# Two-layer decoder trunk: distance tables of the dilated heads loaded one head ahead, latent low parts held behind the first head's scores

## The chip, the cores and the metric

The kernel runs on one core of a Trainium2 chip, in one launch. The metric is the device time of one execution in microseconds, the median of three runs. A profile is one further execution that the hardware profiler recorded; its times are used for the working, the median for the comparison.

## The reference

Two layers, each with a hybrid token mixer, a cross-attention into 256 memory tokens and a squared-ReLU MLP, on 512 tokens of 1024 features in f32. Only the mixer is touched by the change. It projects the normed tokens once and uses the columns for two groups of heads:

```python
z = h @ w_in
c_q, c_kv, k_rope = z[..., :o1], z[..., o1:o2], z[..., o2:o3]    # 384, 256 and 32 columns: "latent"
q_d, k_d, v_d = z[..., o3:o4], z[..., o4:o5], z[..., o5:]        # 512 columns each: "dilated"
q = (rms_norm(c_q, q_norm_g) @ w_uq)                             # 8 latent heads, rope on 32 of 96 columns
kv = (rms_norm(c_kv, kv_norm_g) @ w_ukv)
k_pe = rope(k_rope, positions)                                   # shared by the 8 latent heads
o_mla = causal_block_attention(q, k, v_mla)
for window, dil in ((128, 1), (512, 4), (2048, 16)):             # 8 dilated heads
    s = q_d . k_d * scale + rel_bias[t5_bucket(distance)]        # only the keys of that window and dilation
    o_p, lse_p = softmax(s) @ v_d, logsumexp(s)
o_dil = sum_p softmax_p(lse_p) * o_p
return concat([o_mla, o_dil]) @ w_out
```

## The kernel before

**Numbers.** Every f32 matmul is three fp32r passes: the high part of one operand times the low part of the other, low times high, high times high (L239, L240 and L241). A weight tile `raw`, which SP loads from memory (L157), is therefore split before use: ACT writes the high part `whi` (L192) and VectorE the low part `wlo` as raw minus high (L197). The pools hold 8 raw tiles and 5 each of whi and wlo, so ACT's next `whi` waits until TensorE has done the matmuls of the fifth tile before it.

**The dilated heads.** For a pair of query and key the three dilations together depend on the distance alone, so one table of 128 x 512 per head, `tb`, holds the bias and the count of dilations. The tables are built once, written to memory (`tabw`), and each head loads its own (`dil_table`, L691, 256 KB). `scores` (L460) takes a head in four steps of 128 queries and 128, 256, 384 and 512 keys: TensorE writes `sp` (L467, two passes: keys' high part `kh` and low part `kl`, against a query tile `qs` that holds both parts), VectorE adds the table and takes the row maximum (`P` and `nm`, L471), ACT takes the exponential (L473), VectorE the reciprocal `rs` (L474), POOL scales (L475). There are two PSUM buffers for `sp`, so the third step's matmul waits until VectorE has done the first step. `transposed_scores` transposes P on TensorE (`ptp`, L224), ACT and VectorE copy it out (`PT`, L494 and L492), and `weighted_values` multiplies a pair of heads by the values (`op`, L230).

**The order.** In each layer the q and k columns of the dilated heads are projected feature by feature (`feat_major`, tiles `pfm`; four 128-feature tiles of k, 8 x 3 matmuls each). Each k tile is evacuated for two heads: `kh` on ACT (L637), `kl` on VectorE (L641), and POOL copies both into the other 64 rows (L643). Then `attention()` runs the heads, and `weave` lets the generators `latent()` and `memory()` put their work between its steps, by a ratio of TensorE time: the projection of c_kv and k_rope (`ptm` of 288 columns), of c_q (`ptm` of 384 columns), then the transposes `ctp` and the latent heads' own projections. There are four PSUM buffers for `pfm` and `ptm` together. Within an engine the instructions stand in an order that the scheduler of the compiler's tile framework sets from the program's order and its estimates; `tc.issue_after(x)` makes it put instructions behind x there. All loads stand in one queue of SP, and a load that waits for a free `raw` tile holds those behind it.

Of the kernel before, what the change touches and what calls it, by code (L numbers as in the profile page):

```python
# [11 lines left out]
F32 = mybir.dt.float32  # L12
# [8 lines left out]
S = 512  # L21
# [24 lines left out]
def block_kernel(ctx: ExitStack, tc, x, mem, positions, rel_bias, w_in, q_norm_g, w_uq, kv_norm_g,  # L46
# [11 lines left out]
    sm = ctx.enter_context(tc.tile_pool(name="sm", bufs=40))  # L58
# [109 lines left out]
    def load_w(src, r0, kts, c0, width, gcol=None, heads=0):  # L168
# [18 lines left out]
        for k in range(kts):  # L187
            g = 1.0 if gcol is None else gT[:, gcol + k:gcol + k + 1]
            loads[0] += 1

            with tc.issue_after(token_parts[0]) if 3 <= loads[0] <= 8 else nullcontext():
                weight_parts[:] = [nc.scalar.activation(cols(hi, k, False), cols(raw, k, True), AF.Copy, scale=g).ins]  # L192
            if not SPLIT:
                continue
            lv, rv, hv = cols(lo, k, False), cols(raw, k, True), cols(hi, k, False).bitcast(F32)
            for lv, rv, hv in [(lv[:, e], rv[:, e], hv[:, e]) for e in range(2)] if heads else [(lv, rv, hv)]:
                nc.vector.scalar_tensor_tensor(lv, rv, g, hv, op0=OP.mult, op1=OP.subtract)  # L197
# [256 lines left out]
    OFFS = [0, 128, 384, 768]  # L454

# [3 lines left out]
    def scores(P, parts, tb, scale):  # L459
# [3 lines left out]
        for i in range(NT):  # L463
            L = 128 * (i + 1)
            sp = pss.tile([128, 512], F32, tag="s", name="sp")
            for n, (q, k) in enumerate(parts):
# [4 lines left out]
            nc.vector.tensor_tensor_reduce(out=Pi, in0=sp[:, :L], in1=tb[:, 512 - L:512], scale=-scale,  # L471
                                           scalar=3e38, op0=OP.add, op1=OP.min, accum_out=nm[:, i:i + 1])
# [37 lines left out]
    cs = const.tile([128, NT, 2, ROPE], F32, name="cs")  # L510
    tabd = dr.tile([HEADS, 640], F32, name="tabd")
# [50 lines left out]
    for l in range(DEPTH):  # L562
# [29 lines left out]
        def rope(dst, src, t, n):  # L592

            cosb = cs[:, t, 0:1, :].to_broadcast([128, n, ROPE])
            a = unit("ra")[:, :n * ROPE].rearrange("p (h r) -> p h r", r=ROPE)
            b = unit("rb")[:, :n * ROPE].rearrange("p (h r) -> p h r", r=ROPE)
# [89 lines left out]
        feat_major(wl, o3 + 512, 4, NK, gm, xh_f, xl_f, S, ev_kd, whole=1)  # L686

        def dil_table(h):
            tb = unit("tb")
            src = tabw[h]  # L690
            nc.sync.dma_start(tb, bass.AP(tensor=src.tensor, offset=src.offset + 127, ap=[[639, 128], [1, 512]]))  # L691
            return tb

# [5 lines left out]
        def latent():  # L699
# [3 lines left out]
            yield from tok_major_steps(wl, 0, QL, NK, gm, xh_t, xl_t, NT, ev_cq, whole=True)  # L703
            rq = rstd_from(ssq, QL, "rq")
# [138 lines left out]
        def attention():  # L843

            P, PTs = [None] * 16, [None] * 16
            for i in range(17):
                if i < 8:
                    P[i] = new_scores()
                    yield from scores(P[i], dilated_parts(i), dil_table(i), 1.0)
# [321 lines left out]
```

## Time and profile before

| | |
|---|---|
| median of three runs | 1549.14 us (1545.85 to 1550.41) |
| the profiled execution, its own time | 1551.81 us |
| its span in the trace | 1550.0 us |
| mean granted TensorE clock | 0.989 |
| TensorE, VectorE, ACT, POOL busy | 97%, 64%, 53%, 15% of the span |
| median time of a table from issue to landing | 5.0 us, 16 tables |

Layer 0's dilated heads stand between about 83 and 160 us of the span, layer 1's between about 850 and 925 us. A row of the timeline view gives the start, the duration, the engine, the line and the tile (what is written, `<-`, what is read), and in brackets the idle time of the engine before it with the instruction that ended it. The clock column of a stretch is the share of full speed that the throttle granted TensorE: 1.00 is 2.4 GHz and 0.50 is 1.2 GHz.

### The profile page before, as it was taken

The numbers are of one execution on the slowest core, as the hardware profiler recorded it, in microseconds if no ns is written. First come the engines' busy times: TensorE is split into PE (matmuls) and PEld (weight loads), VectorE is DVE, ScalarE is ACT, GpSimd is POOL, SyncE is SP. The second block draws the span as 40 slices with busy tenths as digits, with TensorE's granted clock in tenths as the row PEclk, the third lists the DMA queues.
The fourth block names the chain that finished last, engine by engine and source line by source line (L and its number), as shares of the span: only waits on it lengthen the run. The fifth ranks groups of instructions, "written<-read, shape, count | busy, mean of one in ns | idle before, by whom it ended". The sixth has DMA issues, their size and how long they took to land.

```text
span 1550.0 us, 21290 instructions
## 1 busy us (share of the span) xinstructions
PE 1509.1 (97%) x7861; PEld 1265.6 (82%) x7861; DVE 995.9 (64%) x1780; ACT 820.0 (53%) x1578; POOL 239.0 (15%) x429
## 2 busy tenths in 40 slices
PE   8999999999999999999989999999999999999996
PEld 7777788898898888888868877978988988888885
DVE  5555775456458668585974667664654594958678
ACT  5355666346346464545554566653553654646363
POOL 2133631021020000000011355201111100000000
PEclk9989999999999999999999999999999999999999
DMA  6432223613131505151541322244322324060612
GB/s 235 143 116 69 79 65 109 204 55 119 53 114 50 181 28 177 41 166 59 179 131 51 122 81 91 69 140 145 109 82 68 115 71 155 17 195 20 190 55 82
DMA packets 87404, 164.09 MB, mean 106 GB/s; under 512 B 6230, under 2 KB 12036, under 8 KB 87300
## 3 DMA queue, kind: packets, MB, share of 16 engines
q1 hardware_dynamic: 86724, 161.68, 32.4%
q8 instruction: 62, 1.02, 0.3%
q10 hardware_dynamic: 576, 1.05, 0.2%
q14 instruction: 42, 0.34, 0.1%
HBM read 154.29 MB, written 11.03 MB: 107 GB/s over the span
## 4 chain that ended last, share of the span: by engine, by line
PE 84%; DVE 7%; issue 3%; ACT 2%; DMA 2%; POOL 1%; SPq 0%; DVEq 0%; POOLq 0%; ACTq 0%
PE pfm L240 12%; PE pfm L239 12%; PE pfm L241 12%; PE ptm L239 6%; PE ptm L240 6%; PE ptm L241 6%; PE wa L239 3%; PE wa L240 3%; PE wa L241 3%; PE sp L467 3%; PE op L230 3%; DVE wlo L197 2%; PE ptp L224 2%; PE wc L240 2%; PE wc L239 2%
## 5 line engine op out<-in xcount | busy, mean ns | idle before, releaser
L240 PE MATMUL pfm<-xth,wlo 128*128 128x512 f32 (+1 forms) x896 | 322.4, 360 | 0.6
L239 PE MATMUL pfm<-xtl,whi 128*128 128x512 f32 (+1 forms) x896 | 322.2, 360 | 0.0
L241 PE MATMUL pfm<-xth,whi 128*128 128x512 f32 (+1 forms) x896 | 321.6, 359 | 0.0
L197 DVE SCALAR_TENSOR_TENSOR wlo<-raw,gT,whi 128x512 fp32r<-128x512 f32 (+3 forms) x332 | 229.1, 729 | 131.6 <-ACT whi L192 129.9
L192 ACT ACTIVATE whi<-raw,gT 128x512 fp32r<-128x512 f32 (+2 forms) x324 | 209.2, 697 | 180.3 <-PE pfm L241 87.3
L164 ACT ACTIVATE whi<-raw 128x1024 fp32r<-128x1024 f32 x112 | 118.1, 1060 | 142.9 <-PE pfm L241 52.8
L240 PEld LDWEIGHTS pfm<-xth,wlo 128*128 128x128 f32 x896 | 169.2, 189 | 26.8 <-DVE wlo L197 1.4
L241 PEld LDWEIGHTS pfm<-xth,whi 128*128 128x128 f32 x896 | 169.2, 189 | 25.6 <-issue 0.5
L239 PEld LDWEIGHTS pfm<-xtl,whi 128*128 128x128 f32 x896 | 169.2, 189 | 24.8
L165 DVE TENSOR_TENSOR wlo<-raw,whi 128x1024 fp32r<-128x1024 f32 x112 | 134.8, 1217 | 34.3 <-ACT whi L164 34.3
L139 POOL TENSOR_TENSOR pnr<-pnm,mhalf 128x1 f32<-128x1 f32 x24 | 18.0, 750 | 828.8 <-DVE pnm L420 828.8
L475 POOL TENSOR_SCALAR P<-P,rs 128x128 f32<-128x128 f32 (+3 forms) x128 | 71.5, 563 | 151.6 <-DVE rs L474 81.2
L239 PE MATMUL wa<-wlo,fh 128*128 128x512 f32 x240 | 93.6, 390 | 0.5 <-DVE acc L1105 0.5
L241 PE MATMUL wa<-whi,fh 128*128 128x512 f32 x240 | 93.4, 389 | 0.0
L240 PE MATMUL wa<-whi,fl 128*128 128x512 f32 x240 | 93.4, 389 | 0.0
L473 ACT ACTIVATE P<-P,nm 128x128 f32<-128x128 f32 (+3 forms) x128 | 71.2, 557 | 34.1 <-DVE nm L471 33.4
L185 DVE TENSOR_TENSOR wlo<-raw,whi 128x1024 fp32r<-128x1024 f32 x32 | 39.1, 1222 | 59.3 <-ACT whi L184 58.6
L239 PE MATMUL ptm<-wlo,xth 128*128 128x512 f32 (+2 forms) x192 | 68.6, 359 | 3.4 <-DVE wlo L197 2.5
L184 ACT ACTIVATE whi<-raw 128x1024 fp32r<-128x1024 f32 x32 | 33.9, 1061 | 67.3 <-PE ptm L241 60.2
L240 PE MATMUL ptm<-whi,xtl 128*128 128x512 f32 (+2 forms) x192 | 67.1, 349 | 0.6 <-DVE xtl L203 0.6
L241 PE MATMUL ptm<-whi,xth 128*128 128x512 f32 (+2 forms) x192 | 66.3, 346 | 0.0
L224 PE MATMUL ptp<-ident,P 128*128 128x128 f32 x320 | 50.5, 282 | 3.9 <-ACT PT L494 2.3
(249 smaller groups left out, 3280.4 us busy)
## 6 DMA issues: line engine op xcount, KB each, us to landing
raw<-in_w_up SPq DMA_DIRECT2D x64, 512.0 KB, 4.6
raw<-in_w_down SPq DMA_DIRECT2D x64, 512.0 KB, 4.3
raw<-in_w_in SPq DMA_DIRECT2D x24, 512.0 KB, 5.5
raw<-in_w_xk SPq DMA_DIRECT2D x16, 512.0 KB, 5.4
raw<-in_w_xv SPq DMA_DIRECT2D x16, 512.0 KB, 3.6
raw<-in_w_mix_out SPq DMA_DIRECT2D x16, 512.0 KB, 4.7
raw<-in_w_xq SPq DMA_DIRECT2D x16, 512.0 KB, 6.4
raw<-in_w_xo SPq DMA_DIRECT2D x16, 512.0 KB, 4.1
```

What stands on the lines that cost most here:

```text
L164: nc.scalar.activation(hi, raw, AF.Copy)
L165: nc.vector.tensor_sub(lo, raw, hi.bitcast(F32))
L192: weight_parts[:] = [nc.scalar.activation(cols(hi, k, False), cols(raw, k, True), AF.Copy, scale=g).ins]
L197: nc.vector.scalar_tensor_tensor(lv, rv, g, hv, op0=OP.mult, op1=OP.subtract)
L224: ins = nc.tensor.transpose(out_, in_, ident_)
L230: nc.tensor.matmul(ps, lhsT=lhsT, rhs=rhs, start=start, stop=stop)
L239: nc.tensor.matmul(ps, lhsT=lh, rhs=rl, start=first, stop=False, skip_group_check=more)
L240: nc.tensor.matmul(ps, lhsT=ll, rhs=rh, start=False, stop=False, skip_group_check=more)
L241: nc.tensor.matmul(ps, lhsT=lh, rhs=rh, start=False, stop=last, skip_group_check=more)
L467: nc.tensor.matmul(sp[:, :L], lhsT=q[:, i * 128:(i + 1) * 128], rhs=k[:, :L], start=n == 0, stop=n == len(parts) - 1)
L473: nc.scalar.activation(Pi, Pi, AF.Exp, bias=nm[:, i:i + 1], scale=-1.0, accum_out=rs[:, i:i + 1])
L475: nc.gpsimd.tensor_scalar(Pi, Pi, rs[:, i:i + 1], 1.0, op0=OP.mult, op1=OP.mult)
```

## The change

Four things, all in the mixer. First, the tables of heads 0 and 1 are loaded ahead of the k projection, and head i (1 to 6) loads the table of head i+1 before its own scores; before, each head loaded its own table ahead of its own scores. Second, from the end of head 0's score steps until the loads of c_q's weights have been put into the program, `behind[0]` holds the last score instruction of head 0, and every `wlo` of a gained weight that is written in that time is put behind it. Third, the rope of the shared key uses a constant tile `rot` instead of two tiles of the pool `un`. Fourth, the pool of small tiles has 34 buffers instead of 40.

```diff
--- before.py
+++ after.py
@@ -55,7 +55,7 @@
     wp = ctx.enter_context(tc.tile_pool(name="wp", bufs=5))
     un = ctx.enter_context(tc.tile_pool(name="un", bufs=39))
     pp = ctx.enter_context(tc.tile_pool(name="pp", bufs=2))
-    sm = ctx.enter_context(tc.tile_pool(name="sm", bufs=40))
+    sm = ctx.enter_context(tc.tile_pool(name="sm", bufs=34))
     psm = ctx.enter_context(tc.tile_pool(name="psm", bufs=4, space=bass.MemoryType.PSUM))
     pss = ctx.enter_context(tc.tile_pool(name="pss", bufs=2, space=bass.MemoryType.PSUM))
     pst = ctx.enter_context(tc.tile_pool(name="pst", bufs=2, space=bass.MemoryType.PSUM))
@@ -194,7 +194,8 @@
                 continue
             lv, rv, hv = cols(lo, k, False), cols(raw, k, True), cols(hi, k, False).bitcast(F32)
             for lv, rv, hv in [(lv[:, e], rv[:, e], hv[:, e]) for e in range(2)] if heads else [(lv, rv, hv)]:
-                nc.vector.scalar_tensor_tensor(lv, rv, g, hv, op0=OP.mult, op1=OP.subtract)
+                with nullcontext() if behind[0] is None else tc.issue_after(behind[0]):
+                    nc.vector.scalar_tensor_tensor(lv, rv, g, hv, op0=OP.mult, op1=OP.subtract)
         return hi, lo
 
     def split_from(hi, lo, src):
@@ -452,6 +453,8 @@
         run(out_proj_steps(*a, **k))
 
     OFFS = [0, 128, 384, 768]
+    score_op = [None]
+    behind = [None]
 
     def new_scores():
         return pp.tile([128, 1280], F32, tag="P", name="P", bufs=2)
@@ -468,8 +471,9 @@
                                  start=n == 0, stop=n == len(parts) - 1)
                 clk[0] += L * (0.00042 if SPLIT else 0.00167)
             Pi = P[:, OFFS[i]:OFFS[i] + L]
-            nc.vector.tensor_tensor_reduce(out=Pi, in0=sp[:, :L], in1=tb[:, 512 - L:512], scale=-scale,
-                                           scalar=3e38, op0=OP.add, op1=OP.min, accum_out=nm[:, i:i + 1])
+            score_op[0] = nc.vector.tensor_tensor_reduce(
+                out=Pi, in0=sp[:, :L], in1=tb[:, 512 - L:512], scale=-scale, scalar=3e38, op0=OP.add,
+                op1=OP.min, accum_out=nm[:, i:i + 1]).ins
             nc.scalar.activation(Pi, Pi, AF.Exp, bias=nm[:, i:i + 1], scale=-1.0, accum_out=rs[:, i:i + 1])
             nc.vector.reciprocal(rs[:, i:i + 1], rs[:, i:i + 1])
             nc.gpsimd.tensor_scalar(Pi, Pi, rs[:, i:i + 1], 1.0, op0=OP.mult, op1=OP.mult)
@@ -508,6 +512,7 @@
         return oh_, ol_
 
     cs = const.tile([128, NT, 2, ROPE], F32, name="cs")
+    rot = const.tile([128, 2, ROPE], F32, name="rot")
     tabd = dr.tile([HEADS, 640], F32, name="tabd")
     tabw = dr.tile([HEADS, 128, 640], F32, name="tabw")
 
@@ -592,8 +597,8 @@
         def rope(dst, src, t, n):
 
             cosb = cs[:, t, 0:1, :].to_broadcast([128, n, ROPE])
-            a = unit("ra")[:, :n * ROPE].rearrange("p (h r) -> p h r", r=ROPE)
-            b = unit("rb")[:, :n * ROPE].rearrange("p (h r) -> p h r", r=ROPE)
+            a, b = (rot[:, 0:1], rot[:, 1:2]) if n == 1 else [
+                unit(name)[:, :n * ROPE].rearrange("p (h r) -> p h r", r=ROPE) for name in ("ra", "rb")]
             nc.gpsimd.tensor_tensor(a, src, cosb, op=OP.mult)
             for e in range(2):
                 nc.gpsimd.tensor_tensor(b[:, :, e * 16:(e + 1) * 16], src[:, :, (1 - e) * 16:(2 - e) * 16],
@@ -683,7 +688,6 @@
             distance_tables()
             rotary_tables()
         feat_major(wl, o3, 4, NK, gm, xh_f, xl_f, S, ev_qd)
-        feat_major(wl, o3 + 512, 4, NK, gm, xh_f, xl_f, S, ev_kd, whole=1)
 
         def dil_table(h):
             tb = unit("tb")
@@ -691,6 +695,10 @@
             nc.sync.dma_start(tb, bass.AP(tensor=src.tensor, offset=src.offset + 127, ap=[[639, 128], [1, 512]]))
             return tb
 
+
+        tables = [dil_table(0), dil_table(1)]
+        feat_major(wl, o3 + 512, 4, NK, gm, xh_f, xl_f, S, ev_kd, whole=1)
+
         ring = [None, None]
         scored = [0]
         keyed, queried = [0], [0]
@@ -701,6 +709,7 @@
             yield from tok_major_steps(wl, QL, KVL + ROPE, NK, gm, xh_t, xl_t, NT, ev_ckv, whole=True)
             rkv = rstd_from(sskv, KVL, "rkv")
             yield from tok_major_steps(wl, 0, QL, NK, gm, xh_t, xl_t, NT, ev_cq, whole=True)
+            behind[0] = None
             rq = rstd_from(ssq, QL, "rq")
             for t in range(NT):
                 nc.vector.tensor_scalar(ckv[t][:, :KVL], ckv[t][:, :KVL], rkv[:, t:t + 1], None, op0=OP.mult)
@@ -846,7 +855,11 @@
             for i in range(17):
                 if i < 8:
                     P[i] = new_scores()
-                    yield from scores(P[i], dilated_parts(i), dil_table(i), 1.0)
+                    if 1 <= i < 7:
+                        tables.append(dil_table(i + 1))
+                    yield from scores(P[i], dilated_parts(i), tables[i], 1.0)
+                    if i == 0:
+                        behind[0] = score_op[0]
                     yield
                 elif i < 16:
                     while min(keyed[0], queried[0]) <= i - 8:
```

What this makes of the order is seen best in three places. The first is ACT in layer 0, from the end of the q projection to the first exponentials of head 0 (`qs` and `kh` are evacuations of the q and k projections, `whi` the high parts of the weights of c_kv, 288 wide, and c_q, 384 wide). Before:

```order
L626 ACTIVATE qs<-pfm 64x512 x3
L637 ACTIVATE kh<-pfm 64x512 x6
L192 ACTIVATE whi<-raw,gT 128x288 x6
L637 ACTIVATE kh<-pfm 64x512
L192 ACTIVATE whi<-raw,gT 128x384 x2
L637 ACTIVATE kh<-pfm 64x512
L192 ACTIVATE whi<-raw,gT 128x384 x6
L473 ACT_TABLE_LOAD
L473 ACTIVATE P,rs<-P,nm 128x128
L473 ACTIVATE P,rs<-P,nm 128x256
```

The same engine at the same place now:

```order
L631 ACTIVATE qs<-pfm 64x512 x3
L192 ACTIVATE whi<-raw,gT 128x288 x6
L192 ACTIVATE whi<-raw,gT 128x384 x2
L642 ACTIVATE kh<-pfm 64x512 x4
L477 ACT_TABLE_LOAD
L477 ACTIVATE P,rs<-P,nm 128x128
L642 ACTIVATE kh<-pfm 64x512
L477 ACTIVATE P,rs<-P,nm 128x256
L477 ACTIVATE P,rs<-P,nm 128x384
L477 ACTIVATE P,rs<-P,nm 128x512
```

The eight `whi` of 288 and 384 columns that stood behind and between the keys' evacuations now stand ahead of all eight `kh`, three of which come after head 0's exponentials; six `whi` of 384 columns, which stood ahead of head 0's exponentials, come later.

VectorE beside it, where `kl` is the keys' low part and `P,nm` the score instruction of head 0. Before:

```order
L628 SCALAR_TENSOR_TENSOR qs<-pfm,qs 64x512 x3
L641 TENSOR_TENSOR kl<-pfm,kh 64x512 x6
L197 SCALAR_TENSOR_TENSOR wlo<-raw,gT,whi 128x288 x6
L641 TENSOR_TENSOR kl<-pfm,kh 64x512
L197 SCALAR_TENSOR_TENSOR wlo<-raw,gT,whi 128x384 x2
L641 TENSOR_TENSOR kl<-pfm,kh 64x512
L197 SCALAR_TENSOR_TENSOR wlo<-raw,gT,whi 128x384 x2
L615 COPY ckv<-ptm 128x288
L197 SCALAR_TENSOR_TENSOR wlo<-raw,gT,whi 128x384 x3
L471 ISA P,nm<-sp,tb 128x128
L471 ISA nm 128x1
L471 ISA P,nm<-sp,tb 128x256
```

And now:

```order
L633 SCALAR_TENSOR_TENSOR qs<-pfm,qs 64x512 x3
L198 SCALAR_TENSOR_TENSOR wlo<-raw,gT,whi 128x288 x6
L646 TENSOR_TENSOR kl<-pfm,kh 64x512 x3
L474 ISA P,nm<-sp,tb 128x128
L474 ISA nm 128x1
L474 ISA P,nm<-sp,tb 128x256
L474 ISA nm 128x1
L646 TENSOR_TENSOR kl<-pfm,kh 64x512
L474 ISA P,nm<-sp,tb 128x384
L474 ISA nm 128x1
L478 RECIPROCAL rs<-rs 128x1
L474 ISA P,nm<-sp,tb 128x512
```

Five low parts of 384 columns stood right ahead of head 0's first score instruction, and two more ahead of those; now the first of them comes behind head 0's last. Three `kl` stand ahead of the first score instruction where all eight stood.

The second place is SP, where `tb` is a table. In layer 0, from the latent heads' up-projection weights (`uq`, `ukv`) to the memory keys' weights (`xk`), before:

```order
L691 DMA tb<-tabw 128x512
L157 DMA raw<-in_w_xk 128x2x512
L691 DMA tb<-tabw 128x512
L157 DMA raw<-in_w_xk 128x2x512 x2
L691 DMA tb<-tabw 128x512 x2
L157 DMA raw<-in_w_xk 128x2x512 x2
L691 DMA tb<-tabw 128x512
L157 DMA raw<-in_w_xk 128x2x512 x2
L691 DMA tb<-tabw 128x512 x2
```

The first `tb` here is head 1's; head 0's stands further ahead. And now, where the first two are those of heads 2 and 3, with heads 0 and 1 further ahead:

```order
L695 DMA tb<-tabw 128x512 x2
L157 DMA raw<-in_w_ukv 128x2x512
L157 DMA raw<-in_w_xk 128x2x512 x3
L695 DMA tb<-tabw 128x512 x2
L157 DMA raw<-in_w_xk 128x2x512 x2
L695 DMA tb<-tabw 128x512
L157 DMA raw<-in_w_xk 128x2x512 x2
L695 DMA tb<-tabw 128x512
L157 DMA raw<-in_w_xk 128x2x512
```

The tables of heads 4 and 5 come behind three loads of `xk`, where head 5's came behind five; those of heads 2 and 3 come ahead of the last `ukv`.

In layer 1 the same stretch, before:

```order
L157 DMA raw<-in_w_uq 128x2x384
L691 DMA tb<-tabw 128x512
L157 DMA raw<-in_w_uq 128x384
L691 DMA tb<-tabw 128x512 x2
L157 DMA raw<-in_w_ukv 128x2x512
L157 DMA raw<-in_w_xk 128x2x512 x3
L691 DMA tb<-tabw 128x512 x2
L157 DMA raw<-in_w_xk 128x2x512 x2
L691 DMA tb<-tabw 128x512
L157 DMA raw<-in_w_xk 128x2x512 x2
```

And now:

```order
L695 DMA tb<-tabw 128x512 x2
L157 DMA raw<-in_w_uq 128x384
L157 DMA raw<-in_w_ukv 128x2x512
L157 DMA raw<-in_w_uq 128x2x384
L695 DMA tb<-tabw 128x512
L157 DMA raw<-in_w_uq 128x384
L695 DMA tb<-tabw 128x512
L157 DMA raw<-in_w_ukv 128x2x512
L157 DMA raw<-in_w_xk 128x2x512 x3
L695 DMA tb<-tabw 128x512 x2
L157 DMA raw<-in_w_xk 128x2x512 x2
```

Head 3's table stood behind `ukv` and three `xk`, and now stands ahead of them (the fourth `tb` of the second piece); head 4's is still behind them.

The third place is TensorE at head 5 of layer 0: `sp` of 384 and 512 keys is the second half of a head's scores, `ctp` the transposes of the latent rows, `ptp` those of P. Before:

```order
L467 MATMUL sp<-kh,qs 128x256
L467 MATMUL sp<-kl,qs 128x256
L224 MATMUL ctp<-ident,ckv 128x128 x4
L224 MATMUL ptp<-ident,P 128x128 x7
L224 MATMUL ctp<-ident,ckv 128x128 x4
L224 MATMUL ctp<-ident,cq 128x128 x4
L467 MATMUL sp<-kh,qs 128x384
L467 MATMUL sp<-kl,qs 128x384
L467 MATMUL sp<-kh,qs 128x512
L467 MATMUL sp<-kl,qs 128x512
L239 MATMUL ptm<-wlo,ch 128x384
L224 MATMUL ctp<-ident,cq 128x128 x4
```

And now:

```order
L470 MATMUL sp<-kh,qs 128x256
L470 MATMUL sp<-kl,qs 128x256
L225 MATMUL ctp<-ident,ckv 128x128 x4
L225 MATMUL ptp<-ident,P 128x128
L470 MATMUL sp<-kh,qs 128x384
L470 MATMUL sp<-kl,qs 128x384
L470 MATMUL sp<-kh,qs 128x512
L470 MATMUL sp<-kl,qs 128x512
L225 MATMUL ptp<-ident,P 128x128 x3
L470 MATMUL sp<-kh,qs 128x128
L470 MATMUL sp<-kl,qs 128x128
L470 MATMUL sp<-kh,qs 128x256
```

The second half of head 5's scores stood behind seven transposes of P and eight of the latent rows, and now stands behind four and one.

## Rows read from the trace of the kernel before

**Rows 1.** Profile page, busy time of each engine, share of the span, instructions
```profile
PE 1509.1 (97%) x7861; PEld 1265.6 (82%) x7861; DVE 995.9 (64%) x1780; ACT 820.0 (53%) x1578; POOL 239.0 (15%) x429
```

**Rows 2.** What PE waited for over the span: total us, times, longest us
```profile
PE sp L467 <- DVE nm L471: 11.4, 11, 1.9
```

**Rows 3.** What VectorE waited for, 85 to 260 us (layer 0), same columns
```profile
DVE P L471 <- DMA tb<-tabw: 2.2, 1, 2.2
```

**Rows 4.** The same for 835 to 935 us (layer 1)
```profile
DVE P L471 <- DMA tb<-tabw: 7.8, 3, 4.1
```

**Rows 5.** Stretches: length, PE, PEld, DVE, ACT, POOL busy, PE clock, DMA share, GB/s
```profile
96.50:98.40 1.90, 0.05 (x2) 0.01 (x1) 1.90 (x7) 1.88 (x3) 0.00 (x0) 1.00 0.57 172
...
99.40:109.60 10.20, 9.20 (x27) 5.91 (x27) 4.50 (x18) 6.04 (x20) 2.09 (x4) 0.50 0.68 214
...
140.00:143.70 3.70, 1.84 (x12) 1.15 (x11) 2.30 (x5) 1.82 (x5) 0.00 (x0) 1.00 0.87 234
143.70:150.60 6.90, 5.52 (x15) 3.71 (x15) 4.20 (x16) 3.47 (x10) 3.12 (x5) 0.51 0.46 179
```

**Rows 6.** ACT in order: start us, us, line, operation, [idle before, releaser]
```profile
67.22 0.59 ACT L637 ACTIVATE kh<-pfm 64x512 fp32r<-64x512 f32 x1 [0.75 <-PE pfm L241]
...
83.48 0.59 ACT L637 ACTIVATE kh<-pfm 64x512 fp32r<-64x512 f32 x1 [0.35 <-PE pfm L241]
83.98 1.11 ACT L192 ACTIVATE whi<-raw,gT 128x384 fp32r<-128x384 f32 x2
...
94.26 3.15 ACT L192 ACTIVATE whi<-raw,gT 128x384 fp32r<-128x384 f32 x6 [8.55 <-issue]
97.42 1.28 ACT L473 ACT_TABLE_LOAD   x1
```

**Rows 7.** VectorE in order, around head 0's first score, same columns
```profile
84.11 0.68 DVE L641 TENSOR_TENSOR kl<-pfm,kh 64x512 fp32r<-64x512 f32 x1 [0.21 <-ACT kh L637]
...
98.05 0.28 DVE L471 CUSTOM_DVE_ANT_0 P<-sp,tb 128x128 f32<-128x128 f32 x1
```

**Rows 8.** POOL in order, 64 to 105 us, same columns
```profile
67.98 0.61 POOL L643 TENSOR_SCALAR kh<-kh 64x512 fp32r<-64x512 f32 x1 [44.10 <-ACT kh L637]
```

**Rows 9.** TensorE in order, third score step of head 0, same columns
```profile
98.39 0.44 PE L467 MATMUL sp<-kh,qs 128*128 128x384 f32 x1 [1.85 <-DVE nm L471]
```

**Rows 10.** TensorE in order, 139 to 152 us, around head 5 of layer 0
```profile
140.79 0.55 PE L224 MATMUL ptp<-ident,P 128*128 128x128 f32 x3 [0.75 <-ACT PT L494]
141.99 0.65 PE L224 MATMUL ctp<-ident,ckv 128*128 128x128 f32 x4 [0.65 <-DVE PT L492]
...
145.08 0.69 PE L467 MATMUL sp<-kh,qs 128*128 128x384 f32 x1 [1.84 <-DVE nm L471]
```

**Rows 11.** DMA issues of SP, 130 to 150 us: start, us, line, tile
```profile
139.63 0.42 SPq L691 DMA_DIRECT2D tb<-tabw  x1
```

**Rows 12.** DMA issues of SP, 872 to 905 us, layer 1
```profile
874.82 4.29 SPq L157 DMA_DIRECT2D raw<-in_w_xk  x3
879.16 0.93 SPq L691 DMA_DIRECT2D tb<-tabw  x2
```

**Rows 13.** VectorE in order, 876:900 us, heads 3, 4, layer 1
```profile
885.29 0.29 DVE L471 CUSTOM_DVE_ANT_0 P<-sp,tb 128x128 f32<-128x128 f32 x1 [4.09 <-DMA tb<-tabw]
...
889.48 0.28 DVE L471 CUSTOM_DVE_ANT_0 P<-sp,tb 128x128 f32<-128x128 f32 x1
```

**Rows 14.** Stretches of layer 1, columns as in Rows 5
```profile
857.00:859.00 2.00, 0.86 (x7) 0.63 (x6) 0.43 (x3) 0.09 (x1) 0.00 (x0) 1.00 1.03 379
...
883.00:886.00 3.00, 1.11 (x9) 0.80 (x8) 0.71 (x5) 0.91 (x3) 0.00 (x0) 1.00 0.44 171
886.00:890.00 4.00, 4.00 (x27) 3.86 (x26) 2.85 (x13) 2.86 (x10) 2.15 (x4) 1.00 0.00 0
902.00:908.30 6.30, 3.33 (x25) 2.43 (x23) 4.16 (x11) 3.24 (x8) 0.00 (x0) 1.00 0.85 282
908.30:911.80 3.50, 3.47 (x13) 3.20 (x13) 3.08 (x12) 2.52 (x8) 1.95 (x4) 0.51 0.57 219
```

## The prediction

> **What bounds the kernel.** I read the profile's page first: TensorE is busy for 97% of the span and VectorE for 64% [rows 1]. So only two things can be won: stretches in which TensorE stands idle, and stretches in which it works at the lower granted clock. The list of waits comes next. TensorE's largest single wait is that of a score matmul for VectorE's `nm`, 11.4 us in 11 waits [rows 2]: with two PSUM buffers for `sp`, the third step of a head starts when VectorE has scored the first. VectorE itself waited for a table once in layer 0, for 2.2 us [rows 3], and three times in layer 1, for 7.8 us [rows 4]. Last I read the timelines around these waits and cut the stretches there, for busy time and clock. The change touches five places.
>
> *Layer 0, head 0.* No table is late here. VectorE has five low parts of c_q's weights ahead of the first score. The last ones need high parts that ACT began at 94.26 after 8.55 us of waiting [rows 6], which is the wait for a free `whi` buffer (the word "issue" names no releaser). So the first score starts at 98.05 [rows 7], and TensorE's third step at 98.39 [rows 9]. In 96.5 to 98.4 TensorE worked 0.05 of 1.90 us, so 1.85 are lost; then for 10.20 us the clock is 0.50, with 9.20 busy [rows 5]. That is 1.00 idle, and 9.20 x 0.50 = 4.60 lost to the clock. Sum 7.45 us.
>
> *Layer 0, head 5.* The table is issued at 139.63 [rows 11] behind five loads of `xk`, VectorE waits 2.2 [rows 3], TensorE 1.84 after it [rows 10]. The stretches 140 to 143.7 and 143.7 to 150.6 lose 1.86 and 1.38 idle, and 5.52 x 0.49 = 2.70 by the clock of 0.51 [rows 5]. Sum 5.94.
>
> *Layer 1.* In the stretch of head 0's wait TensorE stood for 2.00 - 0.86 = 1.14, in that of head 3's for 3.00 - 1.11 = 1.89, both at clock 1.00, and at 1.00 in the 4 us behind head 3's [rows 14]. Around head 5 the loss is 6.30 - 3.33 = 2.97 idle and 3.47 x 0.49 = 1.70 by the clock of 0.51 [rows 14], 4.67 in all.
>
> **The change, part by part.** All terms are microseconds won, against the profiled execution (1551.81, span 1550.0).
>
> *The hold, layer 0, head 0.* The low parts of c_q no longer stand ahead of head 0's score, so the wait of 1.85 and what the clock did behind it go: 7.45 won. But the new order puts eight `whi` ahead of all `kh`. Before, the first `kh` ran at 67.22, while TensorE was still in the k projection [rows 6]. Now the last two `whi` of 384 columns wait for a buffer that the last k matmul sets free; its end is about 83.45, by the `kh` of 83.48 that it released [rows 6]. ACT then needs 1.11 for the two [rows 6], so `kh` starts at about 84.6 and the next one 0.50 later (83.48 to 83.98 [rows 6]). POOL's copy starts 0.76 behind `kh` (67.22 to 67.98) and takes 0.61 [rows 6, 8], so it is done at 86.0; `kl` starts 0.63 behind `kh` (83.48 to 84.11) and takes 0.68 [rows 6, 7], and POOL's copy of it is done at about 86.6. Head 0's first scores need both. What stood behind them on TensorE, the c_kv projection, needs a PSUM buffer that head 1's `kl` sets free, at 86.6 as well. So TensorE, which had no gap here, now stands for 86.6 - 83.45 = 3.1. I bound it by 2.5 (only the first pass waits) and 4.0 (one more evacuation of 0.68 and its neighbour in the way). Behind this gap the clock may fall. The nearest rows are at one end the 4.60 of the old gap, at the other 0, which is what layer 1's head 3 showed behind 1.89 idle [rows 14]. I take 1.70, that of layer 1's head 5, where dense work followed as it does here. Short waits in the new softmax of head 0: the old stretch had 1.00, bounds 0 and 1.00, I take 0.6. Won: 7.45 - (3.1 + 1.7 + 0.6) = 2.0, with ends 7.45 - 2.5 = 5.0 and 7.45 - 9.6 = -2.2.
>
> ACT's table load of 1.28 [rows 6] moves ahead, between the keys' evacuations and the first score's arrival; it costs nothing as long as `kl` and the scores take longer than it. If that cover goes, it is part of the 0.6.
>
> *Tables early, layer 0, head 5.* Its table now stands behind three `xk` loads, where head 4's stood, and VectorE's single wait for a table [rows 3] was not for head 4's. So the 1.84 goes. The waits of 0.75 and 0.65 for copies of P's transposes [rows 10] do not depend on a table and stay, and the scores of heads 5 and 6 now stand closer together, behind the same copies: I charge one more wait of 0.75. Of the clock's 2.70 I count half, since idle time remains just ahead. Won: 1.84 - 0.75 + 1.35 = 2.4; ends 1.84 - 1.40 = 0.4 and 1.84 + 2.70 = 4.5.
>
> *Layer 1.* Head 0: the table is there, but its scores now come ahead of low parts that `ptm` needs next; I take 0, between -1.1 and 1.1. Head 3: its table stood behind three `xk` loads that SP issued at 874.82, and went out at 879.16 [rows 12]; VectorE waited 4.09 for it [rows 13]. Now it goes out ahead of them, so all of TensorE's 1.89 is won; ends 0 and 1.9. Head 5: by the same share as in layer 0 (2.4 of 5.94), 4.67 x 0.41 = 1.9; ends 0 and 4.67 - 1.40 = 3.3.
>
> *The rest.* `rot` changes only where POOL's scratch lies; the POOL instructions are as many, and POOL is busy for 15% [rows 1]. Without that cover it would be one POOL instruction of some 0.6 ahead of `ctp`. The smaller pool of small tiles holds fewer of them alive; I see no instruction that it makes wait. Both 0.
>
> *Sum:* 2.0 + 2.4 + 0 + 1.9 + 1.9 = 8.2. The profiled execution would be 1551.81 - 8.2 = 1543.6. It was 2.67 above the median of the runs, 1549.14, so the forecast is **1540.9 us**. With all upper ends (5.0 + 4.5 + 1.1 + 1.9 + 3.3 = 15.8) it is 1533.3, with all lower ends (-2.9) 1552.0. The forecast's own range is 1537 to 1544.5.
>
> **A rule on the queue.** Head 4's table in layer 1 is still issued behind the three `xk` loads. The row shows the issue at 879.16, and the table of the same issue pair landed at 885.29, 6.1 us later [rows 12, 13]. Head 4's first score started at 889.48 [rows 13], that is 4.2 later. The Trainium skill (page "DMA: Bandwidth & Descriptors", section "Two DMAs through the same engine are not ordered") says that within one queue of one DMA engine the descriptors start in order, so a transfer can't begin ahead of those issued before it. The trace agrees with that by those 6.1 us against the page's median of 5.0; by this rule the time would be that of rival 4 if head 4's scores came over 4.2 earlier, and the forecast if not.
>
> **The rivals.**
> 1. *Nothing takes the place of what goes.* The new gap is at its short end and the clock holds everywhere. For it: layer 1's head 3 kept clock 1.00 behind 1.89 idle [rows 14]. Against it: 3.1 is longer than any gap listed for a score [rows 2]. All upper ends: 1549.14 - 15.8 = 1533.3.
> 2. *The clock makes the new gap as dear as the old one.* For it: 1.85 idle were followed by 10.20 us at 0.50 [rows 5]. Against it: there the work behind was a broken chain of scores, here it is a dense projection. Head 0 becomes 7.45 - (3.1 + 4.6 + 1.0) = -1.25, the rest stays 6.2: 4.95 won, 1544.2.
> 3. *The tables were hidden anyway at head 5.* The copies of P and of the latent rows bind there, and head 5 gives 0.4 in layer 0 and nothing in layer 1, while head 0 gives nothing because its gap eats it: 0.4 + 1.9 = 2.3, so 1546.8. For it: the waits of 0.75 and 0.65 [rows 10]. Against it: a clock of 0.51 behind these gaps [rows 5, 14].
> 4. *The wait moves from head 3 to head 4 in layer 1.* Table 4 lands no earlier; 1.9 less is won: 1542.8. Against it: the 4.2 us of room.
> 5. *Slower: late evacuations hold PSUM.* Five of the keys' evacuations now stand among or behind head 0's exponentials on ACT, and each projection of c_kv's rows needs one of four PSUM buffers that they set free. If the scheduler's estimates are off, TensorE waits there again, for the second and third rows, each time as long as the first (3.1), with the clock at 0.50 in between: 3 x 3.1 + 4.6 + 1.0 = 14.9 against 7.45, and of the rest only 0.4 + 1.9 stays. That is 5.2 lost, 1554.3. It decides once the loss at head 0 passes 7.45 + 6.2 = 13.65. Against it: ACT has two `kh` done ahead of what the first row needs, and 24 matmuls a row to do the next.
>
> **How the numbers follow.** A difference counts as measured above 0.3%, 4.6 us: faster is below 1544.5, slower above 1553.8. Chances: forecast 0.42, rival 1 0.14, rival 2 0.15, rival 3 0.12, rival 4 0.08, rival 5 0.09. Faster: 0.9 of the forecast's, all of rival 1's, half of rival 2's, three quarters of rival 4's, a little of rival 3's, together 0.68. Slower: most of rival 5's, 0.08. The rest, 0.24, is no measurable change. The range takes in rival 1's bound and rival 3 and leaves out rival 5: 1532.5 to 1549.
>
> **What the new profile would show.** Right: TensorE idle for about 3 us at 83.5, no wait of VectorE for `tb` in either layer, the first score of layer 0 near 87 to 88 instead of 98, and 0.50 in the clock for at most some 4 us behind it. Wrong: the k evacuations on ACT before 83 (no new gap), a clock of 0.50 for 10 us behind it (rival 2), score waits of over 1.5 us at head 5 with the table long there (rival 3), or `ptm` waiting for `kl` more than once (rival 5).

## The result, and the profile after

The changed kernel takes **1541.26 us** (six runs, 1540.02 to 1542.40) against 1549.41 of the kernel before in the same comparison: a ratio of 0.9945, with a 95% interval of 0.9935 to 0.9955. The forecast was 1540.9 us, faster. The profiled execution took 1542.40 us with a span of 1540.6, 9.4 us less than before's.

The first rows are TensorE's waits over the whole span (total us, times, longest us); they answer to [rows 2].

```profile
PE sp L470 <- DVE nm L474: 4.5, 10, 0.8
...
PE sp L470 <- POOL kh L648: 2.6, 1, 2.6
```

The score's wait for VectorE fell from 11.4 to 4.5 us; a new one of 2.6 us, for POOL's copy of `kh`, came in. VectorE waits for no table in either layer, where it waited four times [rows 3, 4]. The new wait is the gap at the end of layer 0's k projection; TensorE's timeline there (start, us, line, operation, [idle before, releaser]) answers to [rows 9]:

```profile
88.44 0.50 PE L470 MATMUL sp<-kh,qs 128*128 128x128 f32 x2 [2.64 <-POOL kh L648]
89.09 0.58 PE L470 MATMUL sp<-kl,qs 128*128 128x128 f32 x2 [0.16 <-POOL kl L648]
89.91 0.58 PE L240 MATMUL ptm<-wlo,xth 128*128 128x288 f32 x1 [0.23 <-DVE kl L646]
```

The gap is 2.64 + 0.16 + 0.23 = 3.03 us. VectorE takes head 0's first score at 90.40 us, where it was 98.05 [rows 7]:

```profile
90.40 0.27 DVE L474 CUSTOM_DVE_ANT_0 P<-sp,tb 128x128 f32<-128x128 f32 x1
```

ACT's timeline shows what stood ahead of the keys, as against [rows 6]:

```profile
84.53 0.96 ACT L192 ACTIVATE whi<-raw,gT 128x288 fp32r<-128x288 f32 x2 [0.40 <-ACT whi L192]
85.89 1.12 ACT L192 ACTIVATE whi<-raw,gT 128x384 fp32r<-128x384 f32 x2 [0.40 <-ACT whi L192]
87.03 0.59 ACT L642 ACTIVATE kh<-pfm 64x512 fp32r<-64x512 f32 x1
```

The `whi` come in pairs 1.36 us apart, each pair waiting for a buffer that the projection's matmuls set free; the first `kh` starts at 87.03, 1.2 us behind the projection's end at 85.8, where it ran 16 us ahead of that end before. The stretches of layer 0 (length, then busy time of PE, PEld, DVE, ACT, POOL, then the granted clock) answer to [rows 5]:

```profile
85.80:88.40 2.60, 0.00 (x1) 0.00 (x0) 0.93 (x2) 1.74 (x4) 0.61 (x1) 1.00 0.84 255
...
89.60:92.60 3.00, 2.77 (x12) 2.72 (x12) 2.09 (x7) 2.06 (x3) 2.68 (x6) 0.50 0.00 0
...
97.80:99.00 1.20, 0.62 (x3) 0.30 (x3) 0.13 (x1) 0.59 (x1) 1.11 (x3) 1.00 0.97 325
140.00:143.70 3.70, 3.06 (x18) 2.06 (x17) 3.70 (x16) 3.62 (x12) 1.61 (x3) 1.00 0.77 275
143.70:147.00 3.30, 2.40 (x17) 1.89 (x17) 2.79 (x6) 1.70 (x4) 1.83 (x3) 1.00 0.55 165
147.00:154.00 7.00, 7.00 (x45) 6.37 (x44) 5.57 (x17) 4.97 (x13) 3.82 (x8) 1.00 0.37 116
```

Behind the gap the clock is 0.50 for 3 us instead of 10.2; at head 5 it never leaves 1.00, and 0.64 + 0.90 us are idle where 3.24 were. The same in layer 1, for [rows 14]:

```profile
848.80:866.00 17.20, 17.12 (x125) 16.21 (x124) 12.08 (x46) 12.87 (x38) 11.43 (x28) 1.00 0.32 102
876.00:880.00 4.00, 3.53 (x22) 3.28 (x22) 2.48 (x14) 3.29 (x11) 1.68 (x4) 1.00 0.60 221
898.00:904.00 6.00, 4.57 (x30) 3.34 (x29) 5.38 (x16) 4.39 (x13) 3.44 (x5) 1.00 0.65 218
904.00:908.00 4.00, 4.00 (x26) 3.40 (x25) 2.91 (x11) 3.32 (x9) 1.02 (x3) 1.00 0.60 197
```

Head 0's 1.14 us are gone (0.08 idle in 17.2 us), head 3 has 0.47 left of 1.89, and around head 5 1.43 us are idle where 2.97 were, at full clock.

A sum over each stage, from the end of the k projection to the first 512-column matmul of the memory values' projection, cut into stretches of 1 us, is the account of the whole difference (us; "clock" is busy time times one minus the granted clock):

| stage | before: length, idle, clock | after: length, idle, clock | won |
|---|---|---|---|
| start to the end of layer 0's k projection | 83.45 | 85.80 | -2.35 |
| layer 0's stage | 167.56, 9.34, 7.36 | 161.31, 8.96, 1.58 | 6.25 |
| layer 1's stage | 160.58, 9.16, 1.58 | 155.13, 5.37, 0.00 | 5.45 |
| all between and behind | 1138.41 | 1138.36 | 0.05 |

So in layer 0 the idle time hardly changed and nearly all that was won is clock; in layer 1 two thirds are idle time. That split belongs to these two executions. scratch_only (below) leaves the order of TensorE's instructions as before, and its profiled execution of 1549.28 us lost 1.66 us of clock in layer 0's stage; against it, layer 0 gives 2.35 us and layer 1 6.66. And 2.35 us went at the very start, ahead of the loads and low parts that the change moves: TensorE waited 1.71 us for a low part at 16.6 us, where it had waited 0.52, and the clock was 0.50 from 18 to 20 us.

```profile
16.61 0.50 PE L240 MATMUL ptm<-wlo,xth 128*128 128x512 f32 x1 [1.71 <-DVE wlo L198]
```

### The profile page after: what moved, and what is told of

Read it like the earlier page. It is cut to its first block, busy times and chain, and to the rows that moved or that the text cites. A ratio compares the mean times of both kernels' runs of the same rounds, so it can differ in the third digit from the quotient of the medians.

```text
span 1540.6 us, 21293 instructions
## 1 busy us (share of the span) xinstructions
PE 1504.2 (98%) x7861; PEld 1262.7 (82%) x7861; DVE 996.6 (65%) x1780; ACT 820.6 (53%) x1578; POOL 240.2 (16%) x429
## 4 chain that ended last, share of the span: by engine, by line
PE 81%; DVE 8%; issue 6%; ACT 3%; POOL 1%; DMA 1%; SPq 0%; POOLq 0%; DVEq 0%; ACTq 0%
PE pfm L241 11%; PE pfm L240 11%; PE pfm L242 11%; PE ptm L240 6%; PE ptm L241 6%; PE ptm L242 6%; PE wa L240 3%; PE wa L242 3%; PE wa L241 3%; PE sp L470 3%; PE op L231 3%; PE ptp L225 2%; DVE wlo L198 2%; PE wc L240 2%; PE wc L242 2%
## 5 line engine op out<-in xcount | busy, mean ns | idle before, releaser
L240 PEld LDWEIGHTS wa<-wlo,fh 128*128 128x128 f32 x240 | 45.0, 188 | 10.6 <-DVE acc L1118 1.4
```

Of the source, the lines that this page charges most:

```text
L240: nc.tensor.matmul(ps, lhsT=lh, rhs=rl, start=first, stop=False, skip_group_check=more)
```

## The experiments

Theory A is the prediction's reading: the hold wins what head 0 of layer 0 lost, and by the same stroke makes the gap. Theory B came from the order of the instructions: it is the place of the first two table loads in the program that lets the scheduler put the softmax of heads 0 and 1 beside the c_kv projection, gap included, and the hold does little. Each median stands beside runs of the kernel before on the same chip (1549.81 us for the first four kernels, 1550.66 for the next four, 1550.43 for the last two).

| kernel | median us | ratio to before, 95% interval | layer 0's stage: length, idle, clock | layer 1's |
|---|---|---|---|---|
| hold_only | 1551.58 | 1.002 [1.001, 1.003] | 164.69, 10.17, 2.78 | 162.72, 9.74, 3.42 |
| tables_only | 1540.34 | 0.9941 [0.9927, 0.9954] | 160.26, 8.50, 1.62 | 155.48, 5.77, 0.00 |
| tables_after_k | 1542.86 | 0.9956 [0.9944, 0.9968] | 160.92, 8.27, 1.50 | 156.75, 6.67, 0.00 |
| keys_between | 1538.08 | 0.9926 [0.9914, 0.9938] | 159.45, 8.68, 0.00 | 155.21, 5.36, 0.00 |
| after_again | 1541.36 | 0.9941 [0.9927, 0.9955] | 161.51, 9.05, 1.67 | 155.12, 5.38, 0.00 |
| first_two | 1546.95 | 0.998 [0.997, 0.9991] | 163.52, 9.93, 4.53 | 159.50, 7.68, 2.79 |
| scratch_only | 1549.56 | 0.9999 [0.9987, 1.001] | 163.66, 9.85, 1.66 | 161.79, 9.29, 3.02 |
| keys_between_l0 | 1538.83 | 0.9926 [0.9912, 0.994] | 160.36, 8.39, 1.71 | 155.54, 5.79, 0.00 |
| gap_filled | 1538.55 | 0.9933 [0.9916, 0.9951] | 159.83, 6.48, 0.00 | 155.20, 5.38, 0.00 |
| look_ahead_only | 1542.88 | 0.9959 [0.9948, 0.997] | 162.85, 8.20, 3.36 | 156.37, 6.38, 0.00 |

**hold_only.** The changed kernel with each head's own table again:

```diff
-        tables = [dil_table(0), dil_table(1)]
-                    if 1 <= i < 7:
-                        tables.append(dil_table(i + 1))
-                    yield from scores(P[i], dilated_parts(i), tables[i], 1.0)
+                    yield from scores(P[i], dilated_parts(i), dil_table(i), 1.0)
```

> The hold and the scratch edits alone; every head loads its own table as before. In the order of the instructions the keys' evacuations stand ahead of the weights' high parts again, and heads 0 and 1 of layer 0 are scored behind the c_kv projection. Theory A (the hold wins what head 0 of layer 0 lost, as the prediction priced it): 7.45 us won there, less what takes its place, and nothing elsewhere: 1542 to 1545 us. Theory B (it is the early tables that let the scheduler put the softmax of heads 0 and 1 beside the c_kv projection, and the hold alone only takes the low parts away, while six high parts still stand ahead of the exponentials on ACT): TensorE runs the scores early but waits for the transposes of P at about 100 us as before, clock 0.5 behind it; 0 to 2 us won, 1547.5 to 1549.5 us. No gap at the end of the k projection in either.

It is 0.2% slower than before, so theory A falls: the hold alone wins nothing. Theory B's time is missed as well: it had 0 to 2 us won, and 1.8 were lost. ACT's timeline and, below it, TensorE's say why nothing is won at head 0:

```profile
94.31 3.15 ACT L192 ACTIVATE whi<-raw,gT 128x384 fp32r<-128x384 f32 x6 [8.55 <-issue]
97.48 1.28 ACT L477 ACT_TABLE_LOAD   x1
98.77 0.40 ACT L477 ACTIVATE P<-P,nm 128x128 f32<-128x128 f32 x1
```

```profile
99.99 0.33 PE L225 MATMUL ptp<-ident,P 128*128 128x128 f32 x1 [1.89 <-POOL P L479]
```

No low part stands ahead of the score any more, but on ACT the six high parts still do, waiting 8.55 us for a buffer as before; the exponential starts at 98.77 and TensorE waits 1.89 us for the transposes of P instead of 1.85 us for the score.

**tables_only.** Without the two lines that set `behind[0]` behind head 0:

> The early tables and the scratch edits without the hold. In the order, the high parts of c_kv's weights stand ahead of the keys' evacuations, as in the changed kernel, and no low part stands between the first scores; two low parts of 384 columns stand ahead of the first kl. Theory A (the hold wins at head 0): the loss of 7.45 us at head 0 stays, heads 3 and 5 win 6.2: 1543 us or more, with VectorE's first score of layer 0 near 98 us. Theory B (the early tables do it): first score near 91 us, a gap of about 3 to 3.6 us behind the k projection, 1541.5 to 1542.5 us, that is within 1.5 us of the changed kernel.

1540.34 us, as fast as the changed kernel or a little faster; the gap is there without the hold (TensorE's row first, then VectorE's timeline):

```profile
86.09 0.50 PE L470 MATMUL sp<-kh,qs 128*128 128x128 f32 x2 [2.63 <-POOL kh L648]
```

```profile
84.19 1.15 DVE L198 SCALAR_TENSOR_TENSOR wlo<-raw,gT,whi 128x384 fp32r<-128x384 f32 x2 [0.48 <-ACT whi L192]
85.37 0.68 DVE L646 TENSOR_TENSOR kl<-pfm,kh 64x512 fp32r<-64x512 f32 x1
...
88.11 0.27 DVE L474 CUSTOM_DVE_ANT_0 P<-sp,tb 128x128 f32<-128x128 f32 x1
```

Two low parts stand ahead of the first `kl`; they end at 85.34 as it can start, and cost nearly nothing (the gap is 2.63 us there and 2.64 in the changed kernel). The first score is at 88.11, 4.7 us behind the end of the k projection at 83.45, where it is 4.6 in the changed kernel (the 91 us and the 1541.5 us of the expectation were too late). That is theory B.

**tables_after_k.** One line moved:

```diff
-        tables = [dil_table(0), dil_table(1)]
         feat_major(wl, o3 + 512, 4, NK, gm, xh_f, xl_f, S, ev_kd, whole=1)
+        tables = [dil_table(0), dil_table(1)]
```

> The changed kernel with one line moved: the tables of heads 0 and 1 are loaded behind the k projection in the program instead of ahead of it. SP's queue is almost the same; in the order the keys' evacuations stand ahead of the high parts, and heads 0 and 1 are scored behind the c_kv projection. Theory A (the gap of 3 us behind the k projection comes from the hold): gap unchanged, 1541.3 us. Theory B (gap and early softmax both come from where these two loads stand in the program): no gap at the end of the k projection, but 5 to 8 us lost around 97 to 110 us to idle time and a clock of 0.5, against 5 lost at that place now; heads 3 and 5 as in the changed kernel: 1542 to 1544.5 us.

1542.86 us, in theory B's range. No gap behind the k projection; TensorE's wait stands at 100.94 instead, for the transposes of P:

```profile
100.94 0.33 PE L225 MATMUL ptp<-ident,P 128*128 128x128 f32 x1 [1.89 <-POOL P L479]
```

Around it the idle time is 13.00 - 10.17 = 2.83 us and the clock's loss over the stage 1.50, less than the 5 to 8 that were expected there:

```profile
97.00:110.00 13.00, 10.17 (x49) 7.20 (x48) 8.43 (x38) 11.69 (x34) 7.27 (x18) 0.87 0.11 37
```

Of layer 0's stage the two places of the loads cost the same (160.92 against 161.31 us). Layer 1's is 1.6 us longer: without the early loads head 0's table is late there, as it was before, and TensorE waits 0.93 and then 0.40 us. VectorE's first score of head 0 in layer 1, before and, in the second fence, here:

```profile
858.57 0.29 DVE L471 CUSTOM_DVE_ANT_0 P<-sp,tb 128x128 f32<-128x128 f32 x1 [1.74 <-DMA tb<-tabw]
```

```profile
851.94 0.29 DVE L474 CUSTOM_DVE_ANT_0 P<-sp,tb 128x128 f32<-128x128 f32 x1 [1.27 <-DMA tb<-tabw]
```

**keys_between.** In `load_w`, with a counter over the weights of the latent queries and keys:

```diff
+                if (m, a) == (0, 1):
+                    keys_out[:] = [kh, 0]       # in ev_kd: the second evacuation of the keys
-            with tc.issue_after(token_parts[0]) if 3 <= loads[0] <= 8 else nullcontext():
+            held = token_parts[0] if 3 <= loads[0] <= 8 else keys_out[0] if 6 <= keys_out[1] < 16 else None
+            keys_out[1] += 1
+            with tc.issue_after(held) if held is not None else nullcontext():
```

> The changed kernel, with the last two 288-column high parts and the 384-column ones put behind the first two evacuations of the keys on ACT. Theory B: the gap behind the k projection is ACT's waiting for buffers that the projection's end sets free; with two kh ahead of that wait the gap shrinks from 3.0 to about 0.9 us and the 2.9 us at low clock behind it (1.4 lost) go too: 3 to 3.5 us won, 1537.8 to 1538.3 us. Rival: the gap is set by POOL's copies or by the PSUM buffers that later kl set free, and stays at 2 us or more: 1540.5 to 1541.5 us.

1538.08 us, faster than both kernels and in its time as expected, though not by the stage alone: 1.86 us come from the stage, and in its profile the k projection ended 2.6 us sooner than in the changed kernel's (83.20 against 85.80). This kernel keeps the hold. ACT evacuates both halves of the first k tile ahead of the last `whi` of 288 columns, and TensorE's gap shrinks to 0.16 + 0.32 us (ACT's timeline, then TensorE's):

```profile
80.56 0.96 ACT L194 ACTIVATE whi<-raw,gT 128x288 fp32r<-128x288 f32 x2 [0.40 <-ACT whi L194]
81.55 0.59 ACT L645 ACTIVATE kh<-pfm 64x512 fp32r<-64x512 f32 x1
82.89 0.59 ACT L645 ACTIVATE kh<-pfm 64x512 fp32r<-64x512 f32 x1 [0.75 <-DVE kl L651]
```

```profile
83.62 0.50 PE L473 MATMUL sp<-kl,qs 128*128 128x128 f32 x2 [0.16 <-POOL kl L653]
84.43 0.37 PE L242 MATMUL ptm<-wlo,xth 128*128 128x288 f32 x1 [0.32 <-DVE kl L651]
```

The clock stays at 1.00 in the whole stage. Of the 1.86 us by which the stage is shorter than the changed kernel's, 1.58 are clock and only 0.28 idle time: the idle time of the gap came back further on, where the softmax of head 0 now waits for VectorE's score (0.65 us) and for POOL's scaling (0.60 and 1.34 us).

**after_again, first_two, scratch_only, keys_between_l0.** after_again is the changed kernel itself. first_two loads only the first two tables early, without the hold. scratch_only has only `rot` and the smaller pool. keys_between_l0 is keys_between without the hold and in layer 0 alone.

```diff
# first_two
-                    if 1 <= i < 7:
-                        tables.append(dil_table(i + 1))
+                    if i >= 2:
+                        tables.append(dil_table(i))
# keys_between_l0
+                if l == 0 and (m, a) == (0, 1):
```

> The changed kernel unchanged, beside the others of this call, to compare it with the tables alone (1540.3 us) and to see how far its start varies: 1540 to 1542.5 us. If the wait of TensorE for a low part at 15 us, which made the k projection end 2.35 us later in its first profile than in that of before, belongs to the run and not to the kernel, the k projection ends between 83.2 and 84.5 us here; if it belongs to the change, at about 85.8 us again.

The k projection ended at 85.98 again, so by that expectation the late start goes with this kernel as built. SP's order is the same in the first 45 loads of all kernels. The kernels without the hold ended the k projection at 83.1 to 83.8 us, but so did three with it (83.2, 83.4 and 83.5), and a fourth, tables_after_k, at 84.4. Why this one is late stays open.

> Only the tables of heads 0 and 1 ahead of the k projection; the other six are loaded by their own heads, and no hold. Theory B (these two loads set where heads 0 and 1 of layer 0 are computed, the look-ahead of the others sets heads 3 and 5, and the two add up): layer 0's head 0 as in the changed kernel (2 to 2.5 us won with the gap of 3 us), layer 1's head 0 without its 1.14 us, and the waits for tables at head 5 of layer 0 and heads 3 and 5 of layer 1 back at 1.6 to 1.9 us each: 1545.5 to 1547 us. Rival (the two early tables already push the queue far enough for all): 1541 to 1543 us.

As theory B had it, 1546.95. VectorE's waits for tables are back, in layer 0 and (second fence) layer 1, where they were 2.2 and 7.8 us [rows 3, 4]:

```profile
DVE P L474 <- DMA tb<-tabw: 4.5, 2, 2.7
```

```profile
DVE P L474 <- DMA tb<-tabw: 5.0, 2, 3.0
```

> Only the constant rotary scratch and the smaller pool of small tiles: every theory says no change, 1549 to 1550 us (the order differs in nothing that waits). Over 1 us of difference would mean that the scratch tiles held a buffer that something waited for.

No change, as expected. But its profile tells something of the clock. TensorE's instructions stand in the same order as before, head 0 of layer 0 has the same wait of 1.85 us, and yet the 10 us behind it look otherwise than in [rows 5]:

```profile
96.90:98.80 1.90, 0.04 (x2) 0.02 (x1) 1.90 (x7) 1.88 (x3) 1.64 (x4) 1.00 0.55 161
99.80:110.00 10.20, 8.38 (x41) 5.54 (x41) 6.53 (x30) 8.22 (x27) 5.33 (x16) 1.00 0.75 242
```

The clock stays at 1.00, its loss over the stage is 1.66 us against before's 7.36, and the stage is 3.9 us shorter (163.66 against 167.56). So 3.9 us of what before's profile shows there belonged to that one execution. Head 0 itself lost 1.86 + 1.82 = 3.7 us in these two stretches, where before's profile has 7.45.

> The early tables, no hold, and in layer 0 alone the last two 288-column and the 384-column high parts behind the first two evacuations of the keys. Theory B: layer 0's stage as with keys_between (159.5 us from the end of the k projection to the output projection), layer 1's as in the changed kernel (155.1 to 155.5 instead of 156.5): 1 us less than keys_between, 1536.5 to 1537.5 us. If the hold does matter once the gap is gone: 1538.5 us or more.

1538.83 us: 1 us less than keys_between was expected and none came, so by its time this falls to the other reading, that the hold matters once the gap is gone. But that 1 us rested on a layer 1 of 156.5 us in keys_between, which began before the k projection had ended; from its end on it is 155.21, and 155.54 here. There was nothing to win in layer 1. In layer 0 this kernel is 0.9 us longer, because the clock fell once, behind a wait of 1.34 us that keys_between has as well without that fall. Whether the missing hold has a part in it, one profile of each doesn't show.

**gap_filled.** Behind the k projection of layer 0:

```diff
+        if l == 0:
+            fill = t_ps("fill")
+            for _ in range(24):
+                tc.keep_in_program_order(nc.tensor.matmul(fill[:, 0:256], lhsT=zeros[:, 0:128], rhs=zeros,
+                                                          start=True, stop=True))
```

> The changed kernel with 24 products of zeros (128x256, bf16, into a PSUM tile that nothing reads) on TensorE right behind layer 0's k projection, where it stands idle for 3 us; nothing waits for them and nothing else moves. If the low clock behind that gap (90 to 93 us, 1.6 to 1.7 us lost in four profiles) comes from the idle time ahead of it, the clock stays at 1.00 there and the stage from the k projection's end to the output projection is 1.6 us shorter (159.7 instead of 161.3 to 161.5), 1539.5 to 1540.5 us in all. If the clock falls for what the engine does behind the gap, nothing changes: 161.3 us and 1541.3 us.

The stage is 159.83 us, as the first of the two had it; the time is 1 us below its range. The stretch of the gap and the one behind it:

```profile
83.60:86.20 2.60, 2.60 (x24) 2.11 (x22) 0.74 (x2) 1.83 (x4) 0.78 (x2) 1.00 0.74 240
...
87.60:90.60 3.00, 3.00 (x21) 2.91 (x22) 2.34 (x9) 2.43 (x5) 2.76 (x5) 1.00 0.00 0
```

The scores and projections are the same and start as long after the k projection as in the changed kernel; only TensorE was not idle in between, and the clock stays at 1.00. So the low clock behind the gap came from the idle time ahead of it. The span of this profile is 3.6 us below that of after_again: 1.7 are this stage, 2.6 a k projection that ended at 83.41 instead of 85.98, and 0.7 go the other way elsewhere. The medians, 1538.55 and 1541.36, are from two sets of runs.

**look_ahead_only.** tables_after_k without the hold:

> Tables one head ahead, but those of heads 0 and 1 behind the k projection, and no hold: seven low parts of c_q again stand ahead of or among head 0's scores in layer 0. Theory B (the look-ahead of heads 2 to 7 carries most of the gain, at head 5 of layer 0 and heads 3 and 5 of layer 1): those three places as in the changed kernel, head 0 of layer 0 idle for about 3 us as before, with a clock of 0.5 behind it or not: 1542 to 1546 us. If the hold is what makes the look-ahead pay: 1547 us or more.

1542.88 us, the same as with the hold (1542.86). Head 0's low parts cost idle time and clock as before (answering to [rows 5]):

```profile
96.70:98.70 2.00, 0.14 (x2) 0.11 (x1) 2.00 (x7) 1.98 (x3) 1.73 (x4) 1.00 0.62 190
99.30:106.50 7.20, 6.91 (x25) 4.88 (x23) 4.97 (x23) 5.97 (x21) 3.65 (x8) 0.55 0.62 210
```

yet heads 3 and 5 are as in the changed kernel. So the look-ahead alone, with no load ahead of the k projection, carries 7.5 us of the 8.2 to 9.3 that the changed kernel won in two comparisons. By the ratios the two parts of the early loads add up: 0.20% in first_two and 0.41% here make 0.61%, and both together won 0.59% in tables_only.

## Why the prediction was right

The forecast missed by 0.4 us. The places were right, head by head; of the terms some were right for the reason given and some by size alone, and one was not in the sum. That the total came so close is luck.

- **Head 0 of layer 0: size right, cause wrong.** The gap of 3.1, the clock's 1.7 and the short waits of 0.6 measured 3.03, 1.58 and 0.58 (0.24 + 0.34), and ACT's evacuations made the gap as worked out. But the step "*The hold, layer 0, head 0.*" put both the win and the gap down to the hold, and the early loads of two tables made them: hold_only has neither, tables_only has both. With the tables early the hold adds nothing that shows (1540.34 us without it, 1541.26 and 1541.36 with it; 1542.88 and 1542.86 in the kernels that load them behind the k projection). The order showed only the sum of the two edits; the edits taken one by one would have told it. And 2.0 won holds against before's profile alone: against the 3.7 us that scratch_only lost at this place, the 5.2 that come are a loss of 1.5.
- **Head 5 of layer 0: too small.** Predicted 2.4, measured 3.24 + 2.70 - 1.54 = 4.4. I left half of the clock loss standing and charged one more wait of 0.75; neither came. Whether the table's arrival or the changed order at this head won it was not tried apart.
- **Layer 1: too small.** Predicted 3.8, measured 5.45. Head 0 gave all of its 1.14: VectorE had waited 1.74 for its table, and I took 0 on account of low parts that then cost nothing. Head 3 gave 1.4 (I took 1.9; 0.47 of the old wait remains, for VectorE's score itself), and head 5 gave 4.67 - 1.43 = 3.2 (I took 1.9), again because the clock did not fall.
- **The start: not in it.** The k projection ended 2.35 and 2.53 us later in the two profiles of this kernel, for a reason that stays open. It cancels most of the 3.5 us (6.25 + 5.45 against 8.2) by which the sum of the other terms was too small. It also moves the signs: the gap stands at 85.8 instead of 83.5, the first score at 90.4 instead of 87 to 88.
- **The base.** The sum was made against an execution whose layer 0 was 3.9 us longer than scratch_only's with the same wait at head 0, by its clock. The correction by the median (2.67) took out about two thirds of that. Right, as far as it went, but not worked out from the stage.

Rival 1 fell with the gap of 3.03 us and the 3 us at 0.50 behind it. Rival 2 (a clock loss of 4.6 behind the gap) did not happen: 1.6 to 1.7 in four profiles. Nor did rival 4: head 4's table in layer 1 was issued behind the three loads and VectorE did not wait for it. SP's issues, and VectorE's first scores of heads 3 and 4:

```profile
855.64 0.38 SPq L695 DMA_DIRECT2D tb<-tabw  x1
...
868.89 5.02 SPq L157 DMA_DIRECT2D raw<-in_w_xk  x3
874.01 0.88 SPq L695 DMA_DIRECT2D tb<-tabw  x2
```

```profile
876.13 0.28 DVE L474 CUSTOM_DVE_ANT_0 P<-sp,tb 128x128 f32<-128x128 f32 x1
...
883.11 0.28 DVE L474 CUSTOM_DVE_ANT_0 P<-sp,tb 128x128 f32<-128x128 f32 x1
```

Head 3's table went out at 855.64 instead of 879.16 [rows 12]; head 4's at 874.01 had 9.1 us until its score. The Trainium skill (page "DMA: Bandwidth & Descriptors", section "Two DMAs through the same engine are not ordered") has the descriptors within one queue of one DMA engine start in order; the trace doesn't conflict with it, for a table that starts behind three loads still had time enough in these 9.1 us. Rival 3 fell with head 5, which gave 4.4 us in layer 0 and 3.2 in layer 1, and rival 5 with `ptm` waiting for `kl` once, for 0.23 us. (Its count is off by one: four of the keys' evacuations on ACT stand among or behind head 0's exponentials, not five.)

## What to carry to other kernels

When two edits reach a scheduler together, read the order that each makes alone before you give either a price: here one moved what the other was credited with. A wait of TensorE can pay twice, in idle time and in the clock behind it. The clock's part differed from run to run by more than the wait itself, so price it from several profiles or as a range. And where TensorE must stand idle for a while, as in the gap here, something that keeps it busy can save the clock behind it: in gap_filled it cost nothing.

## What the runs showed of the hardware

Idle stretches of the same length were followed by very different clocks. After 1.85 us at head 0 of layer 0 TensorE worked 10.2 us at 0.50 in one execution [rows 5] and at 1.00 in another, scratch_only's, with the same order of its instructions there. The 3 us behind the k projection cost 1.58 to 1.71 us of clock in four profiles, in two of them the changed kernel's; filled with 24 products of zeros they cost none. The times of one kernel follow the clock as well: of the 15 executions of the kernel before beside gap_filled the fastest took 1544.95 us at a mean granted clock of 0.995, the slowest 1554.43 at 0.988.
